# Recurrent gates on 64-row halves of the TensorE array, and another form of sqrt(1 - a²), in a hybrid decoder layer

## The chip, the core and the metric

The kernel runs on one core of a Trainium2 chip. The time is the device time of one execution in microseconds. Three runs of the kernel before took 2632.26 to 2636.03 us, with a median of 2634.25 us. TensorE (PE) multiplies matrices, its weight loads are listed apart as PEld, VectorE (DVE) and ScalarE (ACT) work on tiles of 128 partitions, and SyncE (SP) issues most of the DMAs. PE adds its products up in PSUM; the other tiles lie in SBUF.

## The reference

The layer reads x (2048 tokens, width 1024). Two groups of heads read the same normalised input: an RG-LRU group and a state-space group (SSD). Their normalised outputs go through one output projection, and a SwiGLU feed-forward network follows. The change touches the RG-LRU part alone, which the reference computes as

```python
xb = xf.reshape(bsz, T, LRU_BLOCKS, LRU_BLOCK_W)          # 16 blocks of 64 channels
r = sigmoid(einsum("btki,kij->btkj", xb, w_a).reshape(bsz, T, W) + b_a)
i = sigmoid(einsum("btki,kij->btkj", xb, w_x).reshape(bsz, T, W) + b_x)
log_a = -LRU_C * r * softplus(-lam)
a = exp(log_a)
u = sqrt(-expm1(2.0 * log_a)) * (i * xf)
h_t = a_t * h_(t-1) + u_t                                 # along the tokens
```

Each gate is block-diagonal: output channel j of block k sees only the 64 channels of block k.

## The kernel before, in words

Channels lie on partitions, 128 of them (two gate blocks) to a tile, and tokens run along the free dimension. The 2048 tokens are worked on in two blocks b = 0, 1 of 1024. In each block the state-space part comes first, and then eight steps i = 0 to 7 of the RG-LRU part, one for each tile of 128 channels.

A float32 product is made of three matmuls on split operands (`mm3`, lines 136 to 139: high by high, high by low, low by high), each 128 x 512. A step of `lru_proj` is two projections of 48 such matmuls into PSUM tiles named pp (px for the recurrence's input, pg for its gate), with the convolution (`conv`, lines 290 to 303) on ACT and DVE behind. `lru_mix` is a generator: its first part splits lx into lh and ll (lines 377 and 378), and its second part makes the gates and the recurrence. `site` (line 325) runs the pieces of the mix of the step before between the products of the present step.

In the mix each gate j (0 is r, 1 is i) has one PSUM tile pr, named pq, of which there are two buffers. Twelve matmuls fill the two tiles: two gates, two halves hh of 512 tokens, three terms. Their weights are 128 x 128 tiles with two 64 x 64 blocks on the diagonal and zeros beside them: bd holds the high part, bdl the low part, which lies in two tiles named Bt and SM. `gates` (lines 357 to 372) builds them; in block b = 1 it loads and subtracts again, since Bt and SM are used by the state-space part between. Then ACT takes tanh of each pr (line 386; the sigmoid is (1 + tanh)/2), exp for a (line 390), tanh(log a) (line 391) and a² (line 393); DVE forms (a² + 1) tanh(log a) (line 394), which is a² - 1, and bounds it at zero (line 395); ACT takes the square root (line 396); and DVE multiplies, scans along the tokens and multiplies with the output gate (lines 397 to 401). The result is written to DRAM (line 314) and its square added to acc (lines 321 and 322).

Three other users of the pq buffers matter here. In block 0, steps i = 4 and i = 6, `normed` prepares block 1's input: `spread` makes a diagonal on DVE (line 155), PE multiplies it into a pq tile (line 158), and eight DVE instructions (line 580) read it. At the end of block 0 acc is summed over channels by eight 128 x 1 matmuls (line 118). At the end of block 1 the first tiles of the output projection follow: `load_wo` converts weight rows on ACT (line 243) and DVE (line 244) into tiles hx (the first eight rows) and wob (the last eight), `half(gs, 0)` multiplies into a pp tile and `half(gs, 1)` into a pq tile.

The order of each engine's instructions is set by a list scheduler at build time: program order gives the priority, a modelled ready time decides among what is ready, and each engine then runs its list in that order, waiting on semaphores. So a change of lines may reorder instructions elsewhere.

Of the kernel before, what the change touches and what calls it, by code (L numbers as in the profile page):

```python
# [37 lines left out]
_o = 0  # L38
for _n, _w in (("g_pre", 8), ("lcw", 32), ("lcb", 8), ("ba", 8), ("bx", 8), ("lam", 8), ("lon", 8),
               ("scw", 48), ("scb", 12), ("sd", 8), ("son", 8), ("g_ffn", 8)):  # L40
    PK[_n] = (_o, _w)
    _o += _w
# [4 lines left out]
def hybrid_layer(ctx: ExitStack, tc: tile.TileContext, x, xT, w_in, w_dt, pack, heads, rows, wa, wx, w_out, w_gu, w_dn, out):  # L47
# [22 lines left out]
    def par(n, i=0, w=None):  # L70
        o, full = PK[n]
        return pk[:, o + i:o + i + (w or 1)]
# [188 lines left out]
    with ExitStack() as fr:  # L261
# [25 lines left out]
        def wide(name):  # L287
            return tp.tile([P, 2, NC, P], F32, name=name, bufs=2)
# [67 lines left out]

        def gates(b, bd):
            st = wide("L").rearrange("p j (t k) l -> p (j t) k l", k=2)
            v.memset(st, 0.0)
            for j, ww in enumerate((wa, wx)):  # L360
                for h in range(2):
                    a.dma_start(out=st[64 * h:64 * h + 64, :, j, 64 * h:64 * h + 64],
                                in_=ww.rearrange("(t two) i j -> two i t j", two=2)[h])
            if b == 0:
                a.copy(out=bd, in_=st)
            res = []
            for q, z in enumerate(("Bt", "SM")):
                lo = tp.tile([P, 4, 2, P], F32R, name=z, bufs=1)
                qs = slice(4 * q, 4 * q + 4)
                v.tensor_sub(out=lo, in0=st[:, qs], in1=bd[:, qs].bitcast(F32))  # L370
                res.append(lo)
            return res

        def lru_mix(b, i, lx, gl, acc, bdl):
            th = []
            lh, ll = (tl.tile([P, TB], F32R, name="t4", bufs=NT4) for _ in range(2))
            a.copy(out=lh, in_=lx)
            v.tensor_sub(out=ll, in0=lx, in1=lh.bitcast(F32))
            yield
            for j in range(2):  # L380
                pr = pq.tile([P, TB], F32, name="pq")
                for hh in range(2):
                    s = slice(hh * HB, (hh + 1) * HB)
                    mm3(pr[:, s], bd[:, i, j, :], bdl[i // 4][:, i % 4, j, :], lh[:, s], ll[:, s], True, True)
                t = t4()
                a.activation(out=t, in_=pr, func=AF.Tanh, scale=0.5, bias=hb[:, 8 * j + i:8 * j + i + 1])
                th.append(t)
            ci = c2[:, i:i + 1]
            av = t4()
            a.activation(out=av, in_=th[0], func=AF.Exp, scale=ci, bias=ci)  # L390
# [248 lines left out]
        for b in range(NB):  # L639
# [17 lines left out]
            if b == 0:  # L657
                bd = fc.tile([P, 8, 2, P], F32R, name="bd")
                hb = fc.tile([P, 16], F32, name="hb")
                v.tensor_scalar(out=hb, in0=par("ba", 0, 16), scalar1=0.5, scalar2=None, op0=ALU.mult)  # L660
# [4 lines left out]
                v.tensor_scalar(out=c2, in0=c2, scalar1=-4.0, scalar2=None, op0=ALU.mult)  # L665
            nhT = {}
            for i in range(8):
# [34 lines left out]
                stages.append(lru_mix(b, i, *xs, acc, bdl))  # L702
            hT = nhT
# [433 lines left out]
```

## Time and profile before

| | |
|---|---|
| median of 3 runs | 2634.25 us |
| profiled execution | 2635.64 us |
| its span | 2633.8 us |
| PE busy | 2613.7 us (99%) |
| DVE busy | 1852.7 us (70%) |
| ACT busy | 1123.6 us (43%) |
| weight loads (PEld) | 2170.4 us (82%) |

The span is the stretch from the first to the last instruction of the profiled execution. Matmuls are pipelined, so a record of one lasts longer than the distance to the next; what one costs is read from the distance of the starts. Rows of the timeline with the same line, operation and shape that follow each other are drawn together, with their count at the end.

### The profile page before, as it was taken

The page shows a single profiled execution, that of the slowest core. Times are in us where ns is not written, and L with a number is a line of the kernel's source. Part 1 is how long each engine was busy: PE and PEld are TensorE (multiplying, and loading weights), DVE is VectorE, ACT ScalarE, POOL GpSimd, SP SyncE. Part 2 cuts the span into 40 slices and gives each one's busy share as a digit, 9 for nine tenths or more (in the row PEclk, how much of TensorE's full clock was granted, in tenths as well). Part 3 has the DMA queues.
Part 4 walks back from the last instruction along what each step waited for, and adds up shares of the span by engine and source line. Part 5 has one row for each costly group of instructions (what it writes and reads, how often), then busy time and mean ns, then how long its engine had stood idle before and what let it go on. Part 6 is the DMA issues. An engine that isn't in the chain of part 4 may idle for free.

```text
span 2633.8 us, 31866 instructions
## 1 busy us (share of the span) xinstructions
PE 2613.7 (99%) x12360; PEld 2170.4 (82%) x12360; DVE 1852.7 (70%) x2716; ACT 1123.6 (43%) x1340; POOL 1.1 (0%) x8
## 2 busy tenths in 40 slices
PE   9999999999999999999999999999999999999998
PEld 7888888888888887888877888888888888888887
DVE  7997878888777767544478777678767675334676
ACT  6544456754535777332253222234222222322443
POOL 0000000000000000000000000000000000000000
PEclk9999999999999999999999999999999999999999
DMA  5342461223334635543454333235333325444664
GB/s 211 111 131 73 128 201 65 82 88 113 95 96 150 210 96 205 154 136 123 143 196 150 134 104 116 81 121 195 104 100 110 106 92 173 151 139 153 212 245 140
DMA packets 189975, 357.79 MB, mean 136 GB/s; under 512 B 18528, under 2 KB 91616, under 8 KB 189824
## 3 DMA queue, kind: packets, MB, share of 16 engines
q1 hardware_dynamic: 88912, 256.56, 30.3%
q10 hardware_dynamic: 100912, 99.20, 10.8%
q8 instruction: 97, 1.59, 0.2%
q14 instruction: 54, 0.44, 0.1%
HBM read 253.86 MB, written 101.84 MB: 135 GB/s over the span
## 4 chain that ended last, share of the span: by engine, by line
PE 93%; DVE 3%; ACT 2%; DMA 1%; issue 1%; DVEq 0%; ACTq 0%; SPq 0%
PE pf L139 16%; PE pf L138 16%; PE pf L137 16%; PE pp L137 11%; PE pp L139 10%; PE pp L138 10%; PE pq L137 3%; PE pq L138 3%; PE pq L139 3%; PE pq L530 1%; PE pq L542 1%; PE pq L551 1%; DMA t_dr<-L 1%; PE pq L514 1%; DVE t L399 0%
## 5 line engine op out<-in xcount | busy, mean ns | idle before, releaser
L137 PE MATMUL pp<-hx,s_hi 128*128 128x512 f32 x1392 | 548.2, 394 | 1.2 <-ACT hx L243 0.7
L139 PE MATMUL pp<-hx,s_lo 128*128 128x512 f32 x1392 | 545.4, 392 | 0.5 <-DVE s_lo L133 0.5
L138 PE MATMUL pp<-hx,s_hi 128*128 128x512 f32 x1392 | 543.6, 391 | 0.6 <-DVE hx L244 0.6
L132 ACT CAST s_hi<-raw 128x1024 fp32r<-128x1024 f32 (+1 forms) x167 | 170.3, 1022 | 380.2 <-PE pp L138 123.0
L139 PEld LDWEIGHTS pp<-hx,s_lo 128*128 128x128 f32 x1392 | 261.7, 188 | 56.5 <-issue 0.9
L137 PEld LDWEIGHTS pp<-hx,s_hi 128*128 128x128 f32 x1392 | 261.8, 188 | 56.2 <-issue 1.6
L138 PEld LDWEIGHTS pp<-hx,s_hi 128*128 128x128 f32 x1392 | 261.9, 188 | 54.2 <-DVE hx L244 1.0
L139 PE MATMUL pf<-hx,s_lo 128*128 128x512 f32 x704 | 273.9, 389 | 0.7 <-DVE s_lo L133 0.7
L137 PE MATMUL pf<-hx,s_hi 128*128 128x512 f32 x704 | 274.2, 389 | 0.4 <-ACT s_hi L132 0.4
L138 PE MATMUL pf<-hx,s_hi 128*128 128x512 f32 x704 | 273.9, 389 | 0.0
L133 DVE TENSOR_TENSOR s_lo<-raw,s_hi 128x1024 fp32r<-128x1024 f32 (+1 forms) x167 | 198.0, 1187 | 64.1 <-ACT s_hi L132 55.7
L978 DVE TENSOR_TENSOR d_lo<-draw,d_hi 128x1024 fp32r<-128x1024 f32 (+1 forms) x110 | 121.5, 1129 | 171.4 <-ACT d_hi L977 170.1
L132 ACT CAST s_hi<-S 128x1024 fp32r<-128x1024 f32 x86 | 90.3, 1050 | 268.6 <-PE pf L138 247.3
L138 PE MATMUL pf<-d_lo,d_hi 128*128 128x512 f32 x504 | 196.1, 389 | 0.0
L977 ACT CAST d_hi<-draw 128x1024 fp32r<-128x1024 f32 (+1 forms) x110 | 104.9, 980 | 213.5 <-PE pf L138 181.6
L139 PE MATMUL pf<-d_hi,d_lo 128*128 128x512 f32 x504 | 195.9, 389 | 0.0
L137 PE MATMUL pf<-d_hi 128*128 128x512 f32 x504 | 194.6, 389 | 0.0
L139 PEld LDWEIGHTS pf<-hx,s_lo 128*128 128x128 f32 x704 | 132.1, 188 | 28.9 <-DVE s_lo L133 1.6
L137 PEld LDWEIGHTS pf<-hx,s_hi 128*128 128x128 f32 x704 | 132.1, 188 | 28.2 <-ACT s_hi L132 0.9
L138 PEld LDWEIGHTS pf<-hx,s_hi 128*128 128x128 f32 x704 | 132.1, 188 | 27.4
L302 DVE SCALAR_TENSOR_TENSOR lx<-xr,pk,lx 128x1024 f32<-128x1024 f32 x108 | 138.2, 1279 | 10.4 <-ACT lx L299 9.3
L138 PE MATMUL pf<-hy,s_hi 128*128 128x512 f32 x356 | 138.8, 390 | 1.5 <-DVE hy L718 1.4
(339 smaller groups left out, 4518.2 us busy)
## 6 DMA issues: line engine op xcount, KB each, us to landing
raw<-w_gu_dram SPq DMA_DIRECT2D x86, 512.0 KB, 4.2
f_dr<-fo ACTq DMA_DIRECT2D x154, 256.0 KB, 4.5
raw<-w_in_dram SPq DMA_DIRECT2D x72, 512.0 KB, 3.4
draw<-f_dr SPq DMA_DIRECT2D x57, 512.0 KB, 4.3
L<-cs_dr SPq DMA_DIRECT2D x32, 512.0 KB, 5.3
g_dr<-t ACTq DMA_DIRECT2D x32, 512.0 KB, 3.4
raw<-g_dr SPq DMA_DIRECT2D x32, 512.0 KB, 5.0
raw<-h_dr SPq DMA_DIRECT2D x26, 512.0 KB, 4.4
```

Source lines behind the costliest of these rows:

```text
L132: a.copy(out=hi, in_=raw)
L133: v.tensor_sub(out=lo, in0=raw, in1=hi.bitcast(F32))
L137: te.matmul(o, lhsT=wh, rhs=hi, start=start, stop=False)
L138: te.matmul(o, lhsT=wh, rhs=lo, start=False, stop=False)
L139: te.matmul(o, lhsT=wl, rhs=hi, start=False, stop=stop)
L302: v.scalar_tensor_tensor(out=y, in0=xr[:, k:k + TB], scalar=cw(k), in1=y, op0=ALU.mult, op1=ALU.add)
L514: te.transpose(pt[:, c].rearrange("p j d -> p (j d)"), xc[:, c * P:(c + 1) * P], ident)
L530: te.matmul(pst[:, c, :], lhsT=Bt[:, c, :], rhs=xe[:, c].rearrange("p j d -> p (j d)"), start=True, stop=True)
L542: te.matmul(po[:, c, :], lhsT=(sc[:, xi, :] if c == 0 else U[:, c - 1, :]), rhs=C[:, c * P:(c + 1) * P], start=True, stop=True)
L551: te.matmul(py[64 * j:64 * j + 64, c, :], lhsT=xd[:, c, j, :], rhs=L[:, j, c, :], start=True, stop=True)
L977: a.copy(out=hi, in_=r)
L978: v.tensor_sub(out=lo, in0=r, in1=hi.bitcast(F32))
```

## The change

The gate weights of the 16 blocks are kept as 64-row pieces in bd and bdl of [128, 8, 128], both held through the whole run: on partitions 64h to 64h+63 lie, side by side, the two 64 x 64 matrices (of r and of i) of block h of the tile; for h = 1 they are exchanged, so that the outputs of the two blocks land on complementary halves of the partitions. A matmul now contracts 64 rows: the block h = 0 uses rows 0 to 63 of the array and writes tile prs[0], the block h = 1 uses rows 64 to 127 and writes prs[1]. There are twelve matmuls of 128 x 512 in a mix as before, the two h taking turns. Each prs holds r of one block and i of another, so tanh is four ACT instructions of 64 x 1024, and the bias of i comes from a copy with exchanged blocks (bxs).

`gates` is called in block 0 only: block 1 has no DMAs, memset and subtractions for it.

For the square root, 1 - a² = (1 + a)² · (-tanh(log(a)/2)), so sqrt(1 - a²) = (1 + a) · sqrt(-tanh(log(a)/2)). ACT takes tanh with half the factor (ch = c2/2) and the root, DVE multiplies (1 + a) into the input product. The square on ACT goes; DVE has the same number of instructions in a mix.

```diff
-                pr = pq.tile([P, TB], F32, name="pq")
-                for hh in range(2):
-                    s = slice(hh * HB, (hh + 1) * HB)
-                    mm3(pr[:, s], bd[:, i, j, :], bdl[i // 4][:, i % 4, j, :], lh[:, s], ll[:, s], True, True)
                 t = t4()
-                a.activation(out=t, in_=pr, func=AF.Tanh, scale=0.5, bias=hb[:, 8 * j + i:8 * j + i + 1])
+            prs = [pq.tile([P, TB], F32, name="pq") for _ in range(2)]
+            for hh in range(2):
+                s = slice(hh * HB, (hh + 1) * HB)
+                for n, (w, z) in enumerate(((bd, lh), (bd, ll), (bdl, lh))):
+                    for h in range(2):
+                        q = slice(64 * h, 64 * h + 64)
+                        te.matmul(prs[h][:, s], lhsT=w[q, i, :], rhs=z[q, s], start=(n == 0), stop=(n == 2))
...
+                for h in range(2):
+                    q = slice(64 * (h ^ j), 64 * (h ^ j) + 64)
+                    a.activation(out=t[64 * h:64 * h + 64, :], in_=prs[h][q, :], func=AF.Tanh, scale=0.5,
+                                 bias=hb[q, 8 * j + i:8 * j + i + 1])
...
-            a.activation(out=th[0], in_=th[0], func=AF.Tanh, scale=ci, bias=ci)
-            a2 = t4()
-            a.activation(out=a2, in_=av, func=AF.Square)
-            v.scalar_tensor_tensor(out=a2, in0=a2, scalar=1.0, in1=th[0], op0=ALU.add, op1=ALU.mult)
-            v.tensor_scalar(out=a2, in0=a2, scalar1=0.0, scalar2=None, op0=ALU.min)
-            a.activation(out=a2, in_=a2, func=AF.Sqrt, scale=-0.25)
+            t2 = t4()
+            a.activation(out=t2, in_=th[0], func=AF.Tanh, scale=cj, bias=cj)
...
+            v.tensor_scalar(out=t2, in0=t2, scalar1=0.0, scalar2=None, op0=ALU.min)
+            a.activation(out=t2, in_=t2, func=AF.Sqrt, scale=-0.25)
             v.scalar_tensor_tensor(out=th[1], in0=th[1], scalar=1.0, in1=lx, op0=ALU.add, op1=ALU.mult)
-            v.tensor_mul(out=th[1], in0=th[1], in1=a2)
+            v.scalar_tensor_tensor(out=th[1], in0=av, scalar=1.0, in1=th[1], op0=ALU.add, op1=ALU.mult)
+            v.tensor_mul(out=th[1], in0=th[1], in1=t2)
...
                 if i == 0:
-                    bdl = gates(b, bd)
+                    if b == 0:
+                        gates(bd, bdl)
```

The built programs' lists show where instructions stand. The first place is PE's list at the mix of step i = 0 of block 0. Before, one gate tile is filled after the other (t4_2622 is lh, t4_2623 is ll, Bt the low weights):

```order
L139 MATMUL pp_2626<-hx_353,s_lo_2409 128x512
L137 MATMUL pq_2681<-t4_2622,bd_2348 128x512
L138 MATMUL pq_2681<-t4_2623,bd_2348 128x512
L139 MATMUL pq_2681<-t4_2622,Bt_2595 128x512
L137 MATMUL pq_2681<-t4_2622,bd_2348 128x512
L138 MATMUL pq_2681<-t4_2623,bd_2348 128x512
L139 MATMUL pq_2681<-t4_2622,Bt_2595 128x512
L137 MATMUL pq_2690<-t4_2622,bd_2348 128x512
```

After, the two PSUM tiles take turns, and each matmul (line 379) works on 64 rows:

```order
L139 MATMUL pp_2626<-hx_353,s_lo_2413 128x512
L379 MATMUL pq_2681<-t4_2622,bd_2348 128x512
L379 MATMUL pq_2682<-t4_2622,bd_2348 128x512
L379 MATMUL pq_2681<-t4_2623,bd_2348 128x512
L379 MATMUL pq_2682<-t4_2623,bd_2348 128x512
L379 MATMUL pq_2681<-t4_2622,bdl_2349 128x512
L379 MATMUL pq_2682<-t4_2622,bdl_2349 128x512
L379 MATMUL pq_2681<-t4_2622,bd_2348 128x512
```

What moved is the order of the tiles: both are in use from the first matmul, and both are complete only with the last two of the twelve. In the whole of the changed list the 192 gate matmuls stand in 24 runs; 12 of them are whole mixes of twelve.

The second place is the end of block 1, where the last mix meets the start of the output projection. On PE before (pq_7574 belongs to the mix, pp_7463 and pp_7512 are the first halves of two output tiles, wob weights belong to the second halves), the mix's last matmul has 54 rows behind it before the first wob matmul:

```order
L137 MATMUL pp_7463<-hx_7437,s_hi_7214 128x512
L139 MATMUL pq_7574<-t4_7561,SM_6136 128x512
L139 MATMUL pp_7512<-hx_7280,s_lo_7454 128x512
L137 MATMUL pp_7512<-hx_7284,s_hi_7453 128x512
...
L137 MATMUL pp_7512<-hx_7447,s_hi_7453 128x512
L138 MATMUL pp_7512<-hx_7448,s_hi_7453 128x512
L139 MATMUL pp_7512<-hx_7447,s_lo_7454 128x512
L137 MATMUL pq_7696<-wob_7618,s_hi_7220 128x512
L138 MATMUL pq_7696<-wob_7619,s_hi_7220 128x512
L139 MATMUL pq_7696<-wob_7618,s_lo_7221 128x512
```

On PE after (line 379 is the mix):

```order
L138 MATMUL pp_7517<-hx_7453,s_hi_7458 128x512
L139 MATMUL pp_7517<-hx_7452,s_lo_7459 128x512
L379 MATMUL pq_7571<-t4_7566,bd_2348 128x512
L379 MATMUL pq_7570<-t4_7567,bd_2348 128x512
L379 MATMUL pq_7571<-t4_7567,bd_2348 128x512
L379 MATMUL pq_7570<-t4_7566,bdl_2349 128x512
L379 MATMUL pq_7571<-t4_7566,bdl_2349 128x512
L137 MATMUL pq_7702<-wob_7624,s_hi_7224 128x512
L137 MATMUL pq_7799<-wob_7624,s_hi_7464 128x512
L138 MATMUL pq_7702<-wob_7625,s_hi_7224 128x512
L139 MATMUL pq_7702<-wob_7624,s_lo_7225 128x512
L137 MATMUL pq_7702<-wob_7628,s_hi_7224 128x512
```

Five of the mix's matmuls moved behind all products of the first halves; the next row is the first that reads wob. On ACT at the same place before (t4_7572, 7583 and 7586 belong to the mix):

```order
L386 ACTIVATE t4_7581<-pq_7574,hb_2349 128x1024
L390 ACT_TABLE_LOAD
L390 ACTIVATE t4_7583<-t4_7572,c2_2351 128x1024
L243 ACTIVATE wob_7618<-raw_7616,pk_109 128x512
L391 ACTIVATE t4_7572<-t4_7572,c2_2351 128x1024
L393 ACTIVATE t4_7586<-t4_7583 128x1024
L243 ACTIVATE wob_7622<-raw_7616,pk_109 128x512
L243 ACTIVATE wob_7628<-raw_7626,pk_109 128x512
L243 ACTIVATE wob_7632<-raw_7626,pk_109 128x512
L396 ACT_TABLE_LOAD
L396 ACTIVATE t4_7586<-t4_7586 128x1024
```

And on ACT after:

```order
L132 CAST s_hi_7464<-raw_7462 128x1024
L384 ACTIVATE t4_7584<-pq_7570,hb_2350 64x1024
L384 ACTIVATE t4_7584<-pq_7571,hb_2350 64x1024
L384 ACTIVATE t4_7587<-pq_7570,hb_2350 64x1024
L384 ACTIVATE t4_7587<-pq_7571,hb_2350 64x1024
L391 ACTIVATE t4_7591<-t4_7584,ch_2384 128x1024
L392 ACT_TABLE_LOAD
L392 ACTIVATE t4_7590<-t4_7584,c2_2353 128x1024
L394 ACT_TABLE_LOAD
L394 ACTIVATE t4_7591<-t4_7591 128x1024
L243 ACTIVATE wob_7624<-raw_7622,pk_109 128x512
L243 ACTIVATE wob_7628<-raw_7622,pk_109 128x512
```

The four tanh, the tanh, the exp and the square root with their two table loads now stand in one piece ahead of the first wob conversion (line 243), which before stood between exp and the second tanh.

The third place is DVE's list in step i = 4 of block 0, around the diagonal of `spread` (line 155). Before (line 399 is the scan):

```order
L308 TENSOR_TENSOR t4_3154<-pp_3099,rsb_143 128x1024
L398 TENSOR_TENSOR t4_3072<-t4_3072,t4_3077 128x1024
L155 TENSOR_TENSOR t4_3163<-ident_113,rtok_144 128x512
L399 SCALAR_TENSOR_TENSOR t4_3072<-t4_3074,hc_147,t4_3072 128x1024
L580 SCALAR_TENSOR_TENSOR L_3157<-L_3157,pk_109,pq_3165 128x512
```

After (line 398 is the scan):

```order
L397 TENSOR_TENSOR t4_3075<-t4_3075,t4_3079 128x1024
L308 TENSOR_TENSOR t4_3157<-pp_3102,rsb_143 128x1024
L398 SCALAR_TENSOR_TENSOR t4_3075<-t4_3078,hc_147,t4_3075 128x1024
L155 TENSOR_TENSOR t4_3166<-ident_113,rtok_144 128x512
L399 COPY hc_147<-t4_3075 128x1
L400 TENSOR_TENSOR t4_2968<-t4_3075,t4_2968 128x1024
```

The scan moved ahead of the diagonal. The same is seen in step i = 6.

## Rows read from the trace of the kernel before

**Rows 1.** The page: busy time per engine (share, count), and the chain's shares by engine

```profile
PE 2613.7 (99%) x12360; PEld 2170.4 (82%) x12360; DVE 1852.7 (70%) x2716; ACT 1123.6 (43%) x1340; POOL 1.1 (0%) x8
...
PE 93%; DVE 3%; ACT 2%; DMA 1%; issue 1%; DVEq 0%; ACTq 0%; SPq 0%
```

**Rows 2.** Waits of PE: line waited for, us in total, times, longest

```profile
PE pq L514 <- DVE t L546: 1.8, 1, 1.8
...
PE pp L137 <- ACT hx L243: 0.7, 1, 0.7
```

**Rows 3.** Instructions on the gate weights bd: duration min/median/max, first and last start

```profile
L137 PE MATMUL pq<-t,bd x64: 387/389/501, 338.7 to 1005.9; 128*128 128x512 f32 x64
...
L370 DVE TENSOR_TENSOR Bt<-L,bd x2: 1221/1222/1223, 315.7 to 810.2; 128x1024 fp32r<-128x1024 f32 x2
```

**Rows 4.** Timeline of PE around one mix: start, duration, line, operation

```profile
338.73 0.39 PE L137 MATMUL pq<-t,bd 128*128 128x512 f32 x1
...
341.26 0.39 PE L139 MATMUL pq<-t,Bt 128*128 128x512 f32 x1
341.49 0.40 PE L137 MATMUL pp<-hx,s_hi 128*128 128x512 f32 x1
```

**Rows 5.** Timeline of PE, 16 full-array matmuls of 128 columns

```profile
222.53 1.95 PE L530 MATMUL pq<-t,Bt 128*128 128x128 f32 x16
224.24 0.48 PE L137 MATMUL pp<-hx,s_hi 128*128 128x512 f32 x1
```

**Rows 6.** Timeline of PE, entering and leaving 64-column weights

```profile
104.32 0.39 PE L137 MATMUL pp<-hx,s_hi 128*128 128x512 f32 x1
104.64 0.44 PE L551 MATMUL pq<-L,t 128*64 128x128 f32 x4
...
157.63 0.50 PE L137 MATMUL pp<-hx,s_hi 128*128 128x512 f32 x1
157.96 0.40 PE L138 MATMUL pp<-hx,s_hi 128*128 128x512 f32 x1
```

**Rows 7.** Timeline of ACT, last mix of block 1

```profile
1010.96 1.10 ACT L386 ACTIVATE t<-pq,hb 128x1024 f32<-128x1024 f32 x1
...
1013.37 1.24 ACT L390 ACTIVATE t<-t,c 128x1024 f32<-128x1024 f32 x1
1014.52 0.71 ACT L243 ACTIVATE wob<-raw,pk 128x512 fp32r<-128x512 f32 x1
...
1019.16 1.28 ACT L396 ACT_TABLE_LOAD   x1
1020.46 1.06 ACT L396 ACTIVATE t<-t 128x1024 f32<-128x1024 f32 x1
```

**Rows 8.** Timeline of PE where the second pq half product starts

```profile
1021.01 0.39 PE L137 MATMUL pq<-wob,s_hi 128*128 128x512 f32 x1
```

**Rows 9.** Timeline of DVE around the spread of block 0, step 4

```profile
403.96 1.22 DVE L398 TENSOR_TENSOR t<-t,t 128x1024 f32<-128x1024 f32 x1
405.09 0.69 DVE L155 TENSOR_TENSOR t<-ident,rtok 128x512 f32<-128x512 f32 x1
405.69 2.35 DVE L399 TENSOR_TENSOR_SCAN t<-t,hc,t 128x1024 f32<-128x1024 f32 x1
407.95 0.72 DVE L580 SCALAR_TENSOR_TENSOR L<-L,pk,pq 128x512 f32<-128x512 f32 x1
```

**Rows 10.** Windows: busy us (count) of PE, PEld, DVE, ACT, POOL; clock, DMA

```profile
387.90:414.60 26.70, 25.92 (x111) 20.50 (x110) 24.50 (x27) 17.61 (x17) 0.00 (x0) 1.00 0.25 79
980.70:1021.00 40.30, 39.06 (x169) 31.22 (x168) 28.97 (x33) 34.03 (x37) 0.00 (x0) 1.00 0.44 141
```

**Rows 11.** Timeline of PE at the end of block 1's first product, and its clock

```profile
547.51 0.72 PE L118 MATMUL pq<-ones,acc 128*128 128x1 f32 x5 [0.97 <-DVE acc L322]
...
551.19 0.63 PE L138 MATMUL pp<-hx,s_hi 128*128 128x512 f32 x1
551.61 0.63 PE L139 MATMUL pp<-hx,s_lo 128*128 128x512 f32 x1
```

More of the change, by code (lines that the diff above doesn't have):

```diff
@@ L38 @@
 _o = 0
-for _n, _w in (("g_pre", 8), ("lcw", 32), ("lcb", 8), ("ba", 8), ("bx", 8), ("lam", 8), ("lon", 8),
+for _n, _w in (("g_pre", 8), ("lcw", 32), ("lcb", 8), ("ba", 8), ("bx", 8), ("bxs", 8), ("lam", 8), ("lon", 8),
                ("scw", 48), ("scb", 12), ("sd", 8), ("son", 8), ("g_ffn", 8)):
@@ L355, in lru_proj, with gates, lru_mix @@
             return lx, gate_of(pg, AF.Gelu_apprx_tanh, b == 0)
[L357 to L362, printed above, removed]
-                                in_=ww.rearrange("(t two) i j -> two i t j", two=2)[h])
[L364 to L374, printed above, removed]
+        def gates(hi, lo):
+            st = wide("L")[:, 0]
+            for h in range(2):
+                for j, ww in enumerate((wa, wx)):
+                    q = slice(64 * (h ^ j), 64 * (h ^ j) + 64)
+                    a.dma_start(out=st[64 * h:64 * h + 64, :, q],
+                                in_=ww.rearrange("(t two) i j -> two i t j", two=2)[h])
+            a.copy(out=hi, in_=st)
+            v.tensor_sub(out=lo, in0=st, in1=hi.bitcast(F32))
+        def lru_mix(b, i, lx, gl, acc):
             th = []
@@ L379, in lru_mix @@
             yield
+            prs = [pq.tile([P, TB], F32, name="pq") for _ in range(2)]
[5 more added lines that the diff above has]
+                        te.matmul(prs[h][:, s], lhsT=w[q, i, :], rhs=z[q, s], start=(n == 0), stop=(n == 2))
             for j in range(2):
-                pr = pq.tile([P, TB], F32, name="pq")
-                for hh in range(2):
-                    s = slice(hh * HB, (hh + 1) * HB)
-                    mm3(pr[:, s], bd[:, i, j, :], bdl[i // 4][:, i % 4, j, :], lh[:, s], ll[:, s], True, True)
                 t = t4()
-                a.activation(out=t, in_=pr, func=AF.Tanh, scale=0.5, bias=hb[:, 8 * j + i:8 * j + i + 1])
+                for h in range(2):
+                    q = slice(64 * (h ^ j), 64 * (h ^ j) + 64)
+                    a.activation(out=t[64 * h:64 * h + 64, :], in_=prs[h][q, :], func=AF.Tanh, scale=0.5,
+                                 bias=hb[q, 8 * j + i:8 * j + i + 1])
                 th.append(t)
@@ L657, in hybrid_layer @@
             if b == 0:
-                bd = fc.tile([P, 8, 2, P], F32R, name="bd")
+                bd, bdl = (fc.tile([P, 8, P], F32R, name=z) for z in ("bd", "bdl"))
                 hb = fc.tile([P, 16], F32, name="hb")
-                v.tensor_scalar(out=hb, in0=par("ba", 0, 16), scalar1=0.5, scalar2=None, op0=ALU.mult)
+                v.tensor_scalar(out=hb[:, 0:8], in0=par("ba", 0, 8), scalar1=0.5, scalar2=None, op0=ALU.mult)
+                v.tensor_scalar(out=hb[:, 8:16], in0=par("bxs", 0, 8), scalar1=0.5, scalar2=None, op0=ALU.mult)
                 c2 = fc.tile([P, 8], F32, name="c2")
@@ L665, in hybrid_layer @@
                 v.tensor_scalar(out=c2, in0=c2, scalar1=-4.0, scalar2=None, op0=ALU.mult)
+                ch = fc.tile([P, 8], F32, name="ch")
+                v.tensor_scalar(out=ch, in0=c2, scalar1=0.5, scalar2=None, op0=ALU.mult)
             nhT = {}
@@ L701, in hybrid_layer @@
                     wk += 1
-                stages.append(lru_mix(b, i, *xs, acc, bdl))
+                stages.append(lru_mix(b, i, *xs, acc))
             hT = nhT
@@ L1105, in chan @@
     def chan(z):
-        z = z.reshape(-1, z.shape[-1])
+        z = z.reshape(z.shape[0], -1)
         return z.reshape(z.shape[0], -1, P).transpose(2, 1, 0).reshape(P, -1)
@@ L1112 @@
     pack = np.concatenate([chan(z) for z in (
-        i["pre_mix_norm"], i["lru_conv_w"][0], i["lru_conv_b"], i["lru_ba"], i["lru_bx"], i["lru_lambda"],
+        i["pre_mix_norm"], i["lru_conv_w"][0], i["lru_conv_b"], i["lru_ba"], i["lru_bx"],
+        i["lru_bx"].reshape(1, 8, 2, 64)[:, :, ::-1], i["lru_lambda"],
         i["lru_out_norm"], i["ssd_conv_w"][0], i["ssd_conv_b"], sd, i["ssd_out_norm"], i["pre_ffn_norm"])], axis=1)
```

1 line of the change is left out of this document (added).

## The prediction

> **What bounds the kernel now.** I read the page first: PE is busy for 2613.7 of 2633.8 us, DVE for 70%, ACT for 43%, and the chain of work that ended last is PE by 93% [rows 1]. So the time is the number of matmuls times their spacing, plus what PE waits. The list of PE's waits comes next: its longest single wait in the whole run is 1.8 us, and the conversions by ACT (line 243) that feed the output projection hold it for 0.7 us, once [rows 2]. PE is thus not waiting for anybody; a change can take time from its own work, or give it waits that it hasn't had.
>
> The gate matmuls are what the change touches on PE. Lines 137 and 138 have 64 each with the weights bd [rows 3], and mm3's third line has as many again: 192 in 16 mixes of twelve. In a mix that stands alone twelve go from 338.73 to 341.49 us, 2.76 us, so 0.230 each [rows 4]: 44 us in all, the most that this change could ever touch on PE.
>
> **The change, part by part.** *Pairs of halves.* The number of matmuls stays at 192 and each still streams 512 columns. The gain comes only if the matmul on rows 0 to 63 and the one on rows 64 to 127, neighbours in PE's list, run at once. No row shows 64-row halves, so I bound the price of a pair: from above by two streams, 0.46 us, from below by one, 0.23. Could weight loads hold a pair longer? Sixteen full-array matmuls of 128 columns go by in 1.71 us, 0.107 each [rows 5], a pace at which loading, not streaming, must set the spacing; two such loads make 0.214 us, under one stream. I take 0.23: the two write different PSUM tiles and read different partitions, and loading would leave room. A mix of twelve then costs 6 x 0.23 = 1.38 us.
>
> The array also changes its shape. The nearest rows are the state-space part's matmuls with 64-column weights: 0.32 us from the last full product to the first of them, and 0.33 from the first full product behind them to the second, where 0.23 is usual [rows 6]. That is 0.1 on each side, 0.2 for a run in and out. A whole mix so saves 2.76 - 1.38 - 0.2 = 1.18 us. Of the 24 runs 12 are whole mixes: 14.2 us. Three mixes of block 0 are broken into two or three runs: step 3 has two lone matmuls and a run of ten, so 7 slots of 0.23 and 3 changes of shape, and saves 0.55; steps 5 and 7 have runs of two and ten and save 0.98 each: 2.5. The last mix is broken into five runs of 8 slots (99 slots in the kernel): 8 x 0.23 + 5 x 0.2 = 2.84 against 2.76, nothing. Sum: 16.7 us gained.
>
> The Trainium skill, "TensorEngine Tiling (Array Packing)", Key Properties, says that different tiles of the array load and multiply in parallel and that a change of tiling mode drains TensorE. No run here shows the first; rows 6 agree with the second, at 0.1 us a side. The page "TensorE: Matmul & The Clock Gate" of the same skill, Part 3, has four 32-row tiles of 512 columns at 3.07 times the speed rather than 4. By that ratio, 0.77, a pair would run at 1.53 times the speed of a single and cost 0.30, and a mix would save 0.76 rather than 1.18; 96 pairs take 6.7 us more, and the forecast would be 2648, inside its own range below.
>
> *ACT and DVE in a mix.* Four tanh of 64 x 1024 come in the place of two of 128 x 1024. At 1.10 us each [rows 7] that is 2.2 us more if a 64-row instruction lasts as long as a 128-row one; the square goes. So a mix gets about 1.1 us longer on ACT, which is busy for 17.6 of 26.7 us in a step [rows 10]: hidden. On DVE the count is the same. The rebuilding in block 1 that goes (four DMAs, a memset, two subtractions of 1.22 [rows 3]) was on no waiting path, so it counts nothing.
>
> *The spread in block 0.* DVE is busy for 24.5 of 26.7 us in step 3's mix [rows 10]. Before, the diagonal (line 155) ended at 405.78 and the scan of 2.35 us came behind it [rows 9]. After, the scan stands ahead of the diagonal, and PE reaches the product of line 158 waiting for it. PE comes no later than before, so each of the two places (steps 4 and 6) gets up to the scan's 2.35 us. Where PE has also saved a mix it comes earlier, and DVE, which has as much work as before, doesn't: that takes back gains. Bounds: nothing if DVE's chain comes forward by that much, 9 us if both waits are twice the scan. I take 2 x 2.35, 5 us.
>
> *The start of block 1.* The first PSUM tiles of block 1 take the pq buffers of the mix of step 7. A buffer is now free only after the third tanh, not the first or second: one tanh, 1.1 us [rows 7]. Bounds 0 and 2.2.
>
> *The end of block 1.* This is the term that decides. Before, the mix's twelve matmuls were done 54 rows before the first wob product, which came at 1021.01 without a wait [rows 8]; under these rows, over 12 us of products, ACT ran the mix's chain, and slipped the first wob conversion in at 1014.52 between exp and tanh [rows 7]. After, five gate matmuls stand last, and the very next row of PE reads wob and writes a pq buffer. The conversion stands on ACT behind four tanh, the tanh, exp, the root and two table loads, and PE has nothing else to issue. From the last gate matmul: 4 x 1.10 + 1.24 + 1.24 + 1.06 + 2 x 1.28 + 0.71 = 11.2 us by [rows 7], plus 0.39 from a matmul's start to its end, less 0.23 since the first tanh needs only the last but one: 11.4, of which 0.3 would pass anyway. PE stands for 11.1 us. Then the low parts come from DVE, whose list has the multiply (1.22), a conversion (some 0.72), the scan (2.35), a conversion, a multiply and a conversion [rows 9]. PE needs the first 12.4 us after the last gate matmul and reaches it at 11.65; the second comes at 15.5 and is reached at 13.55; the third at 17.6, reached at 17.1. That is 0.75 + 1.95 + 0.5 = 3.2 us. Before this, ACT takes mix 6's chain in one piece ahead of the hx conversions: PE, busy for 39.06 of the 40.3 us there before [rows 10], may wait 0 to 4 more; I take 2. And the clock: at 547.51 PE had waited 0.97 us and then done 128 x 1 products, and by 551.19 the spacing was 0.42 us, the lower of the two levels, 1.2 GHz, before it came back [rows 11]. After 11 us without a matmul I expect the same for a few products: 1 us, bounds 0 and 4. Sum 17.3, bounds 14 and 22.
>
> *The sum,* against the profiled execution's 2635.64: -16.7 + 5 + 1.1 + 17.3 = +6.7, 2642.3. The median of the runs is 1.4 lower than that execution, so 2641.
>
> **The rivals.**
> *The halves run one after the other.* For it: no row shows two matmuls at once. Then 192 matmuls stay at 0.23, and 24 runs cost 0.2 each, 4.8 us. PE reaches the spread no earlier, so 2.4 there; 1.1 and 17.3 stay. Sum +25.6: 2660. Against it: the alternation of rows and of PSUM tiles, and loads at 0.107.
> *Faster: the array changes its shape for nothing.* If the lone 0.1 us of rows 6 belong to 64-column weights and not to halves, and a pair streams in the 0.21 us that two loads need [rows 5], all 99 slots cost 20.8 us against 192 x 0.23 = 44.2: 23.4 gained. With the end at its lower bound of 14 and the spread at 2.4, 23.4 - 14 - 2.4 - 1.1 = 5.9 faster: 2628. It decides once the gain is over 22.8 us (14 + 2.4 + 1.1 + 5.3). Against it: the first and the last product around every change of shape in this trace were late.
> *No difference.* The gain is as forecast, the spread's waits don't show since DVE gets free earlier, and the end costs 14 to 16: -16.7 + 1 + 15.5, within a microsecond: 2634. For it: DVE has some 2 us free in a step.
> *The chain on ACT at the end doesn't hold PE,* because a 64-row tanh takes half as long: it takes 2.2 off the end, to 2639, which is still above.
>
> **How the numbers follow.** A measurement of this kernel tells a change of about 0.2%, 5.3 us, from none: 2629.0 to 2639.5 is the same. Forecast: 0.55, its own range 2636 to 2650 by the bounds of the end, the spread and the clock. Halves in turn: 0.17, at 2654 to 2662. Faster: 0.13, 2622 to 2629. No difference: 0.15. A fifth of the forecast, with the fast 64-row tanh, lies under 2639.5. So slower is 0.44 + 0.17, less a little for the edges: 0.58; same 0.15 + 0.11 and those edges, 0.28; faster 0.14. The range reaches from 2628 to 2658.
>
> **What would show it.** In the changed profile: starts of the gate matmuls in pairs, twelve in 1.4 to 1.6 us (right), or 2.8 (halves in turn). A wait of PE of 10 to 12 us on wob (line 243) near 1020 us, the longest of the run, and three shorter ones behind it. PE's waits at line 158 of 2 to 5 us. If PE's wait at wob is under 6 us, the term that makes the forecast is wrong; if the windows of the steps of block 1 are not about 1.2 us shorter each, the gain is.

## The result: 0.9% slower, and where the time went

The changed kernel took 2658.1 us (median of 4 runs, 2657.39 to 2658.56), the kernel before 2634.56 us in the same session. The ratio is 1.0091, with a 95% interval of 1.0076 to 1.0106. The forecast was 2641 us in a range of 2628 to 2658: the direction was right, the loss 23.5 us and not 6.5.

First the page of the changed kernel: busy times, and the chain by engine.

```profile
PE 2613.9 (98%) x12360; PEld 2156.4 (81%) x12360; DVE 1849.0 (70%) x2713; ACT 1145.1 (43%) x1356; POOL 1.1 (0%) x8
...
PE 90%; DVE 4%; ACT 4%; issue 1%; DMA 0%; ACTq 0%; DVEq 0%; SPq 0%
```

Against [rows 1], PE's busy time is the same to 0.2 us, although the gate matmuls got cheaper in most mixes; its share fell, because the span grew by 22.5 us. ACT and DVE have taken part of the chain. Busy time that stays while work shrinks means that other matmuls lasted longer; the clock further down shows which. The list of PE's waits (line waited for, us in total, times, longest) shows the rest:

```profile
PE pq L137 <- ACT wob L243: 11.2, 1, 11.2
PE pq L158 <- DVE t L155: 5.5, 2, 2.9
PE pp L182 <- DVE hx L172: 4.6, 5, 1.7
PE pp L137 <- ACT lx L299: 2.3, 1, 2.3
...
PE pq L421 <- ACT t L384: 0.7, 1, 0.7
```

In [rows 2] the longest wait was 1.8 us. Now one wait of 11.2 us stands at the first wob product; the spread (line 158) and a convolution (line 299) have waits that were not there, and the first product of block 1 (line 182) waits 4.6 us instead of 0.8. All of PE's waits add up to 33.7 us, before to 11.9.

The matmuls themselves did what they were meant to. The mix of step 0 on PE (start, duration, line, operation; equal neighbours drawn together):

```profile
336.65 0.39 PE L139 MATMUL pp<-hx,s_lo 128*128 128x512 f32 x1
336.97 0.73 PE L379 MATMUL pq<-t,bd 64*128 64x512 f32 x4
337.54 0.39 PE L379 MATMUL pq<-t,bdl 64*128 64x512 f32 x2
337.77 0.63 PE L379 MATMUL pq<-t,bd 64*128 64x512 f32 x4
338.24 0.39 PE L379 MATMUL pq<-t,bdl 64*128 64x512 f32 x2
338.56 0.50 PE L137 MATMUL pp<-hx,s_hi 128*128 128x512 f32 x1
338.90 0.39 PE L138 MATMUL pp<-hx,s_hi 128*128 128x512 f32 x1
```

Twelve gate matmuls go from 336.97 to 338.56, 1.59 us instead of 2.76 [rows 4]. Pairs start together and are 0.23 apart. From the last full product to the first pair it is 0.32 us, from the first pair to the second about 0.33, from the last pair to the next full product 0.32, and from that to the one behind it 0.34. These are four steps of about 0.1 above the usual spacing, 0.4 us for a run, where 0.2 was worked out from [rows 6].

The stages, by the start of the first gate matmul of each mix (times from the span's start):

| from, to | before us | after us | difference |
|---|---|---|---|
| start, mix of step 0 | 338.73 | 336.97 | -1.8 |
| step 0, step 2 (two whole mixes) | 49.16 | 47.15 | -2.0 |
| step 2, step 3 (first spread) | 26.73 | 30.49 | +3.8 |
| step 3, step 4 | 24.81 | 24.62 | -0.2 |
| step 4, step 5 (second spread) | 25.69 | 28.97 | +3.3 |
| step 5, step 6 | 24.85 | 23.99 | -0.9 |
| step 6, block 1's step 0 | 343.24 | 351.91 | +8.7 |
| block 1's step 0, step 6 (six whole mixes) | 147.46 | 141.44 | -6.0 |
| step 6, first wob product | 40.34 | 54.07 | +13.7 |
| first wob product, end of span | 1612.79 | 1616.69 | +3.9 |

Where nothing is in the way, a step is 1.0 us shorter (24.58, now 23.57). Three places lose 33.4 us: the two spreads, the start of block 1 in step 7, and the end of block 1. These are rows of one execution each; how far executions differ is taken up with the spread and step 7 below.

The end of block 1 on PE, and on ACT at the same time:

```profile
1027.80 0.62 PE L379 MATMUL pq<-t,bdl 64*128 64x512 f32 x2
1039.61 1.22 PE L137 MATMUL pq<-wob,s_hi 128*128 128x512 f32 x2 [11.19 <-ACT wob L243]
...
1041.52 0.63 PE L139 MATMUL pq<-wob,s_lo 128*128 128x512 f32 x1
1041.94 0.63 PE L137 MATMUL pq<-wob,s_hi 128*128 128x512 f32 x1
...
1043.83 0.79 PE L138 MATMUL pq<-wob,s_hi 128*128 128x512 f32 x1 [0.40 <-DVE wob L244]
...
1045.47 0.39 PE L138 MATMUL pq<-wob,s_hi 128*128 128x512 f32 x1
1045.70 0.40 PE L139 MATMUL pq<-wob,s_lo 128*128 128x512 f32 x1
```

```profile
1028.26 4.50 ACT L384 ACTIVATE t<-pq,hb 64x1024 f32<-64x1024 f32 x4 [10.98 <-PE pq L379]
...
1037.89 1.06 ACT L394 ACTIVATE t<-t 128x1024 f32<-128x1024 f32 x1
1038.86 1.32 ACT L243 ACTIVATE wob<-raw,pk 128x512 fp32r<-128x512 f32 x2
```

PE started its last gate matmul at 1028.0, ended it at 1028.4 and had nothing to issue until the first wob conversion (line 243) was done, behind four tanh (4.50 us together), the tanh, exp and the root. Before, that conversion stood between exp and the second tanh [rows 7], and the product came without a wait [rows 8]. Behind the wait the matmuls stand 0.42 apart until 1045.47, then 0.23: the lower clock level, 1.2 GHz.

In this execution the clock fell at each of the five places with new waits (line 158 twice, lines 182 and 299, and wob), and once more at line 118, where it fell before too [rows 11]. Three of the windows (after the stretch and its length, busy us and count of PE, PEld, DVE, ACT, POOL; then the granted clock as a share of 2.4 GHz, the DMA share, GB/s):

```profile
403.50:410.30 6.80, 5.96 (x12) 4.09 (x13) 6.80 (x11) 1.06 (x1) 0.00 (x0) 0.50 0.49 154
...
512.70:523.00 10.30, 7.63 (x16) 4.43 (x17) 10.30 (x12) 4.88 (x6) 0.00 (x0) 0.50 0.35 113
...
1031.50:1045.20 13.70, 5.10 (x10) 3.16 (x11) 9.36 (x10) 9.80 (x11) 0.00 (x0) 0.50 0.04 7
```

The six stretches, 41 us in all, hold some 60 matmuls that cost about 0.2 us more each, 12 us; before there was one of 3.4 us with 8 [rows 11]. At the first spread:

```profile
404.35 2.05 PE L158 MATMUL pq<-t,ones 128*128 128x512 f32 x2 [2.93 <-DVE t L155]
...
406.62 0.63 PE L137 MATMUL pp<-hx,s_hi 128*128 128x512 f32 x1
407.04 0.63 PE L138 MATMUL pp<-hx,s_hi 128*128 128x512 f32 x1
```

A wait of 2.9 us, and then 0.42 from matmul to matmul. Before, the diagonal stood ahead of the scan [rows 9], and the product came without a wait:

```profile
405.92 1.10 PE L158 MATMUL pq<-t,ones 128*128 128x512 f32 x2
```

The third place is step 7 of block 0, where PE starts block 1's first product (line 182) while ACT and DVE convert its input:

```profile
513.07 0.79 PE L182 MATMUL pp<-hx,s_hi 128*128 128x512 f32 x1 [1.06 <-DVE hx L172]
...
516.01 0.79 PE L182 MATMUL pp<-hx,s_hi 128*128 128x512 f32 x1 [1.71 <-DVE hx L172]
...
519.68 0.79 PE L137 MATMUL pp<-hx,s_hi 128*128 128x512 f32 x1
```

Before, PE filled the gaps between these conversions with the next product (lines 137 to 139), which needs a PSUM tile pp. In the trace before:

```profile
510.95 0.50 PE L182 MATMUL pp<-hx,s_hi 128*128 128x512 f32 x1 [0.78 <-DVE hx L172]
...
511.52 0.40 PE L139 MATMUL pp<-hx,s_lo 128*128 128x512 f32 x1
```

That tile is free when DVE has read the output gate (line 308). The read in the trace before, then in the trace after:

```profile
503.90 1.22 DVE L308 TENSOR_TENSOR t<-pp,rsb 128x1024 f32<-128x1024 f32 x1
```

```profile
517.67 1.22 DVE L308 TENSOR_TENSOR t<-pp,rsb 128x1024 f32<-128x1024 f32 x1
```

It came 13.8 us later, and the filler began only behind it, at 519.68.

### The profile page after: what moved, and what is told of

Its sections match the earlier page's. It is cut to its first block, busy times and chain, and to the rows that moved or that the text cites. A ratio compares the mean times of both kernels' runs of the same rounds, so it can differ in the third digit from the quotient of the medians.

```text
span 2656.3 us, 31892 instructions
## 1 busy us (share of the span) xinstructions
PE 2613.9 (98%) x12360; PEld 2156.4 (81%) x12360; DVE 1849.0 (70%) x2713; ACT 1145.1 (43%) x1356; POOL 1.1 (0%) x8
## 3 DMA queue, kind: packets, MB, share of 16 engines
q10 hardware_dynamic: 98800, 98.68, 10.7%
q8 instruction: 97, 1.59, 0.3%
## 4 chain that ended last, share of the span: by engine, by line
PE 90%; DVE 4%; ACT 4%; issue 1%; DMA 0%; ACTq 0%; DVEq 0%; SPq 0%
PE pf L139 16%; PE pf L138 16%; PE pf L137 16%; PE pp L137 10%; PE pp L139 10%; PE pp L138 10%; PE pq L138 2%; PE pq L137 2%; PE pq L139 2%; ACT t L384 1%; PE pq L529 1%; PE pq L550 1%; PE pq L541 1%; DVE t L398 1%; PE pq L379 1%
```

## The experiments

Each run is the changed kernel with the edit shown, unless it says otherwise; constants that an edit defines are written as numbers. Before was 2634.4 to 2634.8 us in these sessions.

**The two halves of the change apart.** `g_only` keeps the 64-row gates and takes back the square root:

```diff
-            a.activation(out=t2, in_=th[0], func=AF.Tanh, scale=cj, bias=cj)
...
+            a.activation(out=a2, in_=av, func=AF.Square)
+            v.scalar_tensor_tensor(out=a2, in0=a2, scalar=1.0, in1=th[0], op0=ALU.add, op1=ALU.mult)
```

> One half of the change alone: gates on 64-row halves with weights prepared once, and the square root in the old form, with the square of a on ACT. Theory A (the halves save about 1.0 us per mix, and what lost the time is the order that the new square root gives ACT and DVE): the wait of 11 us at the first wob product isn't there, a mix takes 1.6 us rather than 2.76, steps of block 1 last 23.57 us rather than 24.58, and the kernel takes 2620 to 2628 us, faster than before. Rival (both PSUM tiles of the gates being held at once, and four tanh, make the waits): the waits at line 158, at line 182 and at wob are as in the changed kernel, and the time is 2650 to 2660 us.

`f_only` is the kernel before with the new square root alone (the same lines exchanged the other way).

> The other half of the change alone: full-array gates as before (weights rebuilt in block 1), and the square root in the new form. Theory A: this half brings the waits (the list of PE has the last gate matmuls just ahead of the first wob product again, and ACT the whole chain ahead of the wob conversion) and no gain; two tanh of 128 x 1024 rather than four of 64 make the wait at wob about 9 us: 2648 to 2662 us. Rival (the halves bring the waits): within 5 us of the kernel before.

Measured: `g_only` 2637.4 us (ratio 1.0017, 1.0008 to 1.0027), `f_only` 2646.7 (1.0048, 1.0033 to 1.0063). PE's waits in the first, and in the second:

```profile
PE pp L137 <- ACT lx L299: 4.6, 1, 4.6
PE pq L158 <- DVE t L155: 3.1, 2, 1.7
```

```profile
PE pq L137 <- ACT wob L243: 8.3, 2, 7.9
PE pq L158 <- DVE t L155: 2.1, 2, 1.1
```

The long wait at wob belongs to the new square root: with full-array gates the list has it too, 7.9 us with two tanh. The halves alone have no such wait and steps of 23.57 us, and still didn't win: 4.6 us at the convolution's ACT instruction (line 299) with a low clock from 990.0 to 996.8, and 3 us at the spreads. `g_only` lies 9 us above the upper end of its forecast, `f_only` 1.3 below the lower end. Together the two lose 23.5 us, apart 3 and 12: the row of step 7 (343.24 us before, 351.91 after) is 341.64 in `f_only` and 345.35 in `g_only`, so most of that loss needs both.

**The end.** `e_end` writes the last mix ahead of the first half products.

```diff
-                firsts = {n: half(gq[n], 0) for n in range(2)}
                 while stages:
                     site(3)
+                firsts = {n: half(gq[n], 0) for n in range(2)}
```

> The changed kernel with one edit: at the end of block 1 the last mix is written ahead of the two first half products instead of behind them, so its five late gate matmuls no longer stand between these products and the first wob product. Theory A (the three places where PE waits after a reordering, and the low clock behind each, make the loss; the paired matmuls do give about 1.0 us per mix): the wait of 11.19 us at the first wob product goes to under 1 us, and with it the low clock from 1031.5 to 1045.2; from the first gate matmul of mix 6 to the end the changed kernel took 17.6 us longer than before, and some 2 to 4 of these (the wait on ACT line 299 and its low clock) stay. Forecast 2643 us, 2640 to 2646. Theory B (the mix is simply slower on ACT, four tanh and one piece, and holds the wob conversions wherever it stands): the wait shrinks to 5 us or more, and the time is 2649 to 2654. Theory C (the loss is spread over all mixes): 2655 to 2658.

Measured: 2644.8 us (1.0042, 1.0027 to 1.0057), as theory A had it.

```profile
PE pq L158 <- DVE t L155: 5.5, 2, 2.9
PE pp L182 <- DVE hx L172: 4.6, 5, 1.7
...
PE pq L137 <- ACT wob L243: 0.9, 2, 0.6
```

The wait at wob is 0.9 us in two pieces, with 1.9 more at its low halves (line 244); the waits at the other two places are unchanged. So 13.3 us of the 23.5 were the end's order alone.

**The spread.** `e_spread` gives it a higher priority, which puts the diagonal ahead of the scan.

```diff
-            ps = spread(rtok[:, b], 4 * hh, 4, t4())
+            with tc.high_priority(offset=150):
+                ps = spread(rtok[:, b], 4 * hh, 4, t4())
```

> The changed kernel with one edit: the spread of block 0 (steps 4 and 6) gets a higher priority, which moves the diagonal (line 155) ahead of the scan on DVE, as it stood before. Theory A: the waits of 2.9 and 2.6 us at line 158 shrink by the scan's 2.35 us, and the low clock behind them (403.5 to 410.3 and 458.1 to 461.5 us) goes. From mix 2 to mix 3 the changed kernel took 3.8 us longer than before and from mix 4 to mix 5 3.3, although each should be 1.0 shorter: 7 to 9 us come back, 2650 us. Rival: DVE is so full there that PE waits for the same work one instruction later (line 580's readers, lx, the split), and only the clock's part or nothing comes back: 2655 to 2658.

Measured: 2656.0 us (1.0086, 1.0071 to 1.0101). The two steps took 26.76 and 26.06 instead of 30.49 and 28.97, 6.6 us less in the profile, but the median fell by 2 only. The 6.6 overstate the edit: in `e_end` and `e_step7`, whose lists are those of the changed kernel up to step 7 of block 0, the same two steps took 29.23 and 28.89, and 27.63 and 27.31 us. Against the last pair the edit gives 2.1 us. `e_diag` gives the diagonal a tile of its own and forms it ahead:

```diff
+        dgs = fc.tile([P, 4, P], F32, name="dgs")
...
+            te.matmul(ps[:, 0:HB], lhsT=ones, rhs=dgs.rearrange("p c t -> p (c t)"), start=True, stop=True)
```

> The changed kernel with one edit: the diagonal of the spread has a tile of its own, 2 KB per partition, and is formed long before its product, so that line 158's product depends neither on the scan nor on a working tile that a mix gives back. Theory A (the diagonal's place on DVE behind the scan makes the waits of 5.5 us and the low clock behind them): both waits go, mix 2 to mix 3 takes 24 to 25 us rather than 30.5 and mix 4 to mix 5 about 24 to 25 rather than 29.0, and with the end and step 7 as they were the kernel takes 2646 to 2650. Rival (DVE is full, and PE waits at the next instruction that DVE feeds): steps of 27 us or more, 2653 to 2658.

Measured: 2655.8 us (1.0086, 1.0073 to 1.01). No wait at the spread's product is left, and mix 2 to 3 takes 24.45 us, mix 4 to 5 24.45; but the next steps take 28.13 and 27.08 (before 24.81 and 24.85). PE in step 4, and DVE at the same place:

```profile
413.22 0.49 PE L379 MATMUL pq<-t,bd 64*128 64x512 f32 x1 [1.88 <-DVE L L582]
```

```profile
406.68 2.71 DVE L582 SCALAR_TENSOR_TENSOR L<-L,pk,pq 128x512 f32<-128x512 f32 x4
...
410.44 2.72 DVE L582 SCALAR_TENSOR_TENSOR L<-L,pk,pq 128x512 f32<-128x512 f32 x4
```

The rival has it. The mix of step 3 needs both pq buffers for its first pair, the spread holds one of them, and DVE, busy for all of the 9.2 us from 404.0 to 413.2, reads it eight times (line 582 here, 580 before) between other work until 413.2. The wait moved by one instruction.

**Step 7.** `e_step7` converts block 1's input sooner:

```diff
-                        with tc.high_priority(offset=HQ):
+                        with tc.high_priority(offset=200):
                             build_hT(nhT, xb, 1)
```

> The changed kernel with one edit: the conversion of block 1's second half of the input at the end of step 7 of block 0 gets a higher priority, so that its first piece stands on ACT between the mix's exp and its root, and the others follow sooner. Theory A: the five waits at line 182 (4.6 us) and the low clock from 512.7 to 522.9 us shrink; of the 10 us by which this step is longer than its share, 4 to 9 come back: 2651 us. Rival: the conversions wait for buffers that the last products of block 0 free, not for their place on ACT: nothing comes back, 2656 to 2659.

Measured: 2657.0 us (1.0087, 1.0072 to 1.0102); waits at line 182 of 4.1 instead of 4.6 us. The conversions' place on ACT is not it.

This run shows something else of the clock. Its waits at the spreads' products (line 159 here) are as long as in the changed kernel, 2.92 and 2.60 us, and yet the granted clock from 404 to 411 and from 455 to 462 us is 1.00:

```profile
407.12 1.10 PE L159 MATMUL pq<-t,ones 128*128 128x512 f32 x2 [2.92 <-DVE t L156]
...
408.29 0.39 PE L138 MATMUL pp<-hx,s_hi 128*128 128x512 f32 x1
408.52 0.39 PE L139 MATMUL pp<-hx,s_hi 128*128 128x512 f32 x1
```

The matmuls behind the wait stand 0.23 apart, not 0.42. So the same wait brings the low level in one execution and not in another, and that is most of the 4.5 us by which the two rows of the spreads together differ here from the changed kernel's, with the same lists.

`e_gread` gives priority to the read of the output gate:

```diff
             if scaled:
-                v.tensor_tensor(out=t, in0=ps, in1=rsb, op=ALU.mult)
+                with tc.high_priority(offset=60):
+                    v.tensor_tensor(out=t, in0=ps, in1=rsb, op=ALU.mult)
```

> The changed kernel with one edit: in block 0 the DVE instruction that reads the output gate's PSUM tile (line 308) gets a higher priority. In step 7 it stood at 517.67 us, 12.7 us after its product was done, and held the pp buffer that the next product of block 1 needs, so that PE had nothing to put between its waits at line 182. Theory A: with this read ahead of the scan PE fills these waits, the low clock from 512.7 to 523.0 goes, and 5 to 10 us come back: 2648 to 2653 us; the end of block 1 stays as it was. Rival: the conversions (line 172) hold PE by themselves, 2656 to 2659.

Measured: 2651.7 us (1.0069, 1.0054 to 1.0084). The read (line 310 here) stands ahead of the scan, and of five waits at line 182 (183 here) one is left:

```profile
502.79 1.22 DVE L310 TENSOR_TENSOR t<-pp,rsb 128x1024 f32<-128x1024 f32 x1
503.93 2.34 DVE L400 TENSOR_TENSOR_SCAN t<-t,hc,t 128x1024 f32<-128x1024 f32 x1
```

```profile
PE pp L183 <- DVE hx L173: 1.2, 1, 1.2
```

Step 6 to block 1's step 0 takes 343.65 us instead of 351.91, 8.3 less; the median fell by 6.4. The PSUM tile held by a late read was the cause of most of the loss there. The edit moves this read in every step of block 0, so the median doesn't price step 7 alone; the row does.

**Together.** `e_all` has the edits of `e_end`, `e_spread` and `e_step7`.

> The three edits together in the changed kernel. Theory A: the gains add up, 15 + 8 + 6 us: 2629 us (2624 to 2636), so under the kernel before by some of what the paired matmuls save (about 1.0 us in each of 16 mixes). Rival (what is gained at one place is lost at the next, since DVE and ACT have no more room): 2640 us or more. Rival (the pairs save nothing by themselves and the reordering is all): 2634 to 2640 with steps of block 1 as long as before, 24.6 us.

Measured: 2643.4 us (1.0033, 1.0019 to 1.0048), 14.7 less than the change, little more than the end's part; step 6 to block 1's step 0 still took 351.2. `e_reads` has the end, the spread, and priority for every read of the projections' PSUM tiles (the gate's, as above, and the convolution's two).

> The changed kernel with four edits: the last mix ahead of the first half products, the spread earlier, and a higher priority for all instructions that read the projections' PSUM tiles (the output gate's and the convolution's). Theory A: the losses at the end, at step 7 and at the conversion of line 299 go together, and what is left is the gain of the halves less two or three us at the spreads: 2624 to 2634 us, faster than before or equal. Rival (ACT and DVE have no room, so each thing put first delays another): 2640 us or more, as with the three edits before.

Measured: 2635.2 us (1.0002, 0.9992 to 1.0011), equal to before. `e_reads_wob` adds priority for the first four wob rows:

```diff
-        wo += [load_wo(ow2 if k < 14 else ow1, k) for k in range(8, 16)]
+        for k in range(8, 16):
+            with tc.high_priority(offset=400 if k < 12 else 0):
+                wo.append(load_wo(ow2 if k < 14 else ow1, k))
```

> The changed kernel with the last mix ahead, the spread earlier, the PSUM reads first, and the first four wob rows at a higher priority. Without the last of these it took as long as the kernel before, 4.8 us of it lost behind the first wob product, where PE waits for conversions one by one. Theory A: 3 to 5 us of these come back: 2629 to 2633. Rival: the conversions wait for the same DVE, 2634 to 2637.

Measured: 2632.0 us (0.9992, 0.9983 to 1.0001), the lowest of all and still not clear of before. By the rows of the stage table it still gives back some 3 us at the steps with spreads, 3 at the row of step 7 and 5 at the end, against what the pairs save there. `e_half_reads` has the priorities for reads and wob with the old square root, `e_control` has them in the kernel before.

> The halves with the old square root, plus a higher priority for the instructions that read the projections' PSUM tiles (convolution, output gate) and for the first four wob rows. The halves alone lost 4.6 us at the conversion of line 299, a low clock from 990 to 996.8 behind it, and some 4 us at step 7. Theory A: these go, the steps of block 1 stay at 23.57 us, and the time is 2622 to 2630 us, faster than the kernel before. Rival (the room on ACT and DVE is the limit): 2632 to 2640.

> The kernel before, neither half of the change, with the same priorities for PSUM reads and wob rows. Theory A: it has none of these waits, so nothing changes beyond a microsecond or two, 2631 to 2638, and what the run above gains is the halves' own. Rival: the priorities by themselves gain as much as there, under 2630.

Measured: 2641.9 us (1.0025, 1.0015 to 1.0036) and 2636.2 us (1.0002, 0.9994 to 1.0011). The control says that these priorities do nothing by themselves in the kernel before; the edits of the end and the spread were not tried there. The first fell against theory A: the convolution's wait went, but its place was taken by 4.5 us at a conversion for the output projection (line 245) with a low clock from 998.4 to 1015.4. `e_best` is `e_reads_wob` with the diagonal of `e_diag` in place of the spread's priority.

> The same tile for the diagonal, with the last mix ahead, the PSUM reads first and the first four wob rows at a higher priority. That kernel without the tile took 2632.0 us, and waited 3.4 us at the spread's products. Theory A: these go and the steps 2 to 6 of block 0 get 24 to 25 us each: 2624 to 2629 us, faster than the kernel before by 0.2 to 0.4%. Rival: the time moves to the next instruction that DVE feeds, 2630 to 2634.

Measured: 2633.8 us (0.9998, 0.9988 to 1.0007). Steps 2 to 3 and 4 to 5 take 24.45 and 24.44 us, steps 3 to 4 and 5 to 6 take 29.79 and 27.15: the rival again.

**Do the halves need to take turns?** `e_serial` issues three matmuls on one half and then three on the other.

```diff
-                for n, (w, z) in enumerate(((bd, lh), (bd, ll), (bdl, lh))):
-                    for h in range(2):
+                for h in range(2):
+                    for n, (w, z) in enumerate(((bd, lh), (bd, ll), (bdl, lh))):
```

> The changed kernel with the two halves no longer taking turns: three matmuls on rows 0 to 63, then three on rows 64 to 127. If a pair runs at once only where neighbours in the list are on different halves, a mix of twelve takes about 2.4 to 2.9 us rather than 1.6, and the steps of block 1 about 24.6 to 24.8 rather than 23.57. If PE pairs them by itself, 1.6 us and 23.6.

One run: 2654.0 us, and the mix is

```profile
338.19 0.73 PE L379 MATMUL pq<-t,bd 64*128 64x512 f32 x4
338.76 0.40 PE L379 MATMUL pq<-t,bdl 64*128 64x512 f32 x2
339.00 0.63 PE L379 MATMUL pq<-t,bd 64*128 64x512 f32 x4
339.46 0.40 PE L379 MATMUL pq<-t,bdl 64*128 64x512 f32 x2
339.79 0.50 PE L137 MATMUL pp<-hx,s_hi 128*128 128x512 f32 x1
```

1.60 us, the same groups with the same gaps as when they take turns: bd and bdl of both halves appear together. PE pairs them by itself, as the second forecast had it. Four of the six whole steps of block 1 take 23.58 us; one takes 26.17 and one 24.00.

## Why the prediction went wrong, by its own steps

- **The pairs and the change of shape.** Right in kind, and too large: a run in and out costs 0.4 us, not 0.2. The steps between the first two pairs and behind the last one are not in [rows 6]. A whole mix so gave 1.0 us and not 1.18, 14.1 us in all (the table's gains, 9.1, and 1.0 for each of the five mixes in rows that lose) rather than 16.7. The rival of halves in turn is refuted, though its 2660 was the nearest number: about the right time for a wrong reason. The Trainium skill, "TensorE: Matmul & The Clock Gate", Part 3, has 3.07 of 4 for four row tiles; here a pair costs the 0.23 us of one matmul, and what is lost is at the ends of a run.
- **The spread.** 5 us forecast, bounds 0 and 9; measured 9.1 (3.8 and 3.3, and the 1.0 that each step should have saved). Waits of 5.5 us were in the sum by their mechanism, the low clock behind them was not: in `e_step7`, with the same waits at the full clock, the two steps cost 0.9 and 1.6 and the same 2.0, 4.5 us, about the forecast. And `e_diag` shows that the diagonal was only the first in a queue: with DVE full and both pq buffers needed at once, the wait sits in the buffer.
- **The start of block 1: the step that failed.** It was priced at one tanh, 1.1 us, bounds 0 and 2.2. Measured: 8.7 and the 2 us that two mixes should have saved, 10.7. The wait that I priced came, at 0.7 us (line 421, waiting for a tanh of line 384). But I looked at who frees the pq buffers and not at pp, a wait that the sum so put at nothing. The order showed DVE's gate read (line 308) moved behind eleven other instructions in step 7, and I had not followed it; `e_gread` gave 8.3 us of this row back with the priority of that one line.
- **The end of block 1.** Forecast 17.3 us, of which 11.1 a stall at wob; measured 11.19 for the stall and 18.6 in all (13.7, 3.9 and mix 6's 1.0). `e_end` gave 13.3 back. The stall is right; that the sum came out is in part luck, as two misses cancel. The waits for low halves were 0.4 us, not 3.2: PE, at the low clock, came to the first at 1041.52, and its conversion was done at 1040.86. And 18 matmuls at the low clock, behind line 299 and behind wob, cost 3.6 us, not 1.
- **The clock.** Priced at 1 us, at one place, with bounds to 4. In the profiled execution it fell five more times and cost some 10 us: 60 matmuls at 0.2 rather than 8. [rows 11] had it low behind a wait of 1 us; I applied that row once, to the longest wait, and should have given each wait that the change adds a bound for it. Only a bound: `e_step7` kept the full clock behind 2.92 us, and `e_reads_wob` behind 2.04.
- **ACT and DVE in a mix** were called hidden. Four tanh cost 4.50 us, a 64-row one thus 1.12, as the upper bound said. Their busy time was hidden, but a chain without a gap on ACT keeps other readers waiting. The sum had that only at the end of block 1, at line 243 and as 2 us for mix 6's chain; that chain held ACT from 987.80 to 998.41 us, ahead of line 299, for which PE waited 2.3 us.

By the forecast's sums: -14.1 + 9.1 + 10.7 + 18.6 = +24.3, and with the -1.8 of the first 337 us the measured 22.5. This is the stage table in another order and so must add up; it does not test the parts. The -1.8 is no effect of the change that these runs can tell: with the same lists up to there, the first mix began at 338.52 us in `e_end` and at 339.75 in `e_step7`. What tests the parts are the single edits: 13.3 (end), 6.4 (gate read) and 2.1 us (spread, not clear of the noise) of the median, 21.8 of the 23.5; `e_reads`, with all of them and the convolution's reads, gave 22.9 back.

## What to carry to other kernels

When a kernel is bound by one engine with no waits, price a change by the waits that its new order adds: for each PSUM or SBUF tile, find who frees it and where that instruction now stands on its engine. Slow matmuls may follow a new wait on TensorE, here in some executions and not in others, so each new wait is to be priced by itself, with the low clock as its upper bound. A form with fewer instructions on an engine can lose, if the gaps in which others got their turn go with them (`f_only`: 7.9 us at wob).

## What the runs showed of the hardware

Matmuls on rows 0 to 63 and on rows 64 to 127 run at once with 0.23 us a pair, also where the list has three of one half and then three of the other (`e_serial`): the two halves behave like two queues. The Trainium skill, "TensorE: Matmul & The Clock Gate", Part 3, says that matmuls start and end strictly in their order; the mix of `e_serial`, six pairs in 1.60 us, differs, and the measurement decides. A run of halves costs 0.4 us beside the streams, at entry, between the first two pairs and at exit. A tanh on 64 partitions of 1024 elements takes 1.11 us (median of 64), on 128 partitions 1.12 (median of 32). Waits of 2.9 and 2.6 us for the spreads' products were followed by the lower clock level in the changed kernel's profile and by the full one in that of `e_step7`.
